# A streaming GELU-multiply: first tile loaded and stored in two pieces, GELU written to the output tile, whole-tile instructions elsewhere, activations pinned behind stores

## The chip, the cores and the metric

One core of one Trainium2 chip. The metric is the time on the device in microseconds (us), median of several runs; lower is better. The span, from the first to the last instruction, is 1.7 to 2.6 us shorter than the time of the same run.

## The reference

```python
x = randn(32, 512, 2048)  # float32
x1, x2 = x[..., :1024], x[..., 1024:]
gelu_x1 = 0.5 * x1 * (1 + erf(x1 / sqrt(2)))
return gelu_x1 * x2
```

134.2 MB are read and 67.1 MB written, with one GELU and one multiply for each output element.

## The kernel before

The rows are cut into 16 tiles: 128 partitions, 8 rows of 2048 columns each, so 8.39 MB in and 4.19 MB out. Both pools have two buffers. SP's queue issues the loads and the last two tiles' stores; ACT's queue issues the other stores.

```python
def load(i):
    x_tile = xpool.tile([P, R, dim], x.dtype, name="x_tile")
    nc.sync.dma_start(out=x_tile, in_=x_t[i])
    return x_tile
...
ahead = [load(0), load(1)]
for i in range(n_tiles):
    x_tile = ahead.pop(0)
    o_tile = opool.tile([P, R, half], out.dtype, name="o_tile")
    last = i == n_tiles - 1
    for lo, hi in ((0, 1), (1, 2), (2, 4), (4, 8)) if last else ((0, 4), (4, 8)):
        rows = slice(lo, hi)
        nc.scalar.activation(
            out=x_tile[:, rows, :half], in_=x_tile[:, rows, :half], func=GELU
        )
        nc.vector.tensor_mul(
            out=o_tile[:, rows, :],
            in0=x_tile[:, rows, :half],
            in1=x_tile[:, rows, half:],
        )
        if last and hi % 4 == 0:
            store(nc.sync, i, o_tile, slice(hi - 4, hi))
    if not last:
        store(nc.sync if i == n_tiles - 2 else nc.scalar, i, o_tile, slice(0, R))
    if i + 2 < n_tiles:
        ahead.append(load(i + 2))
```

A tile framework adds the semaphores, and it may choose the order of instructions on an engine where the data allow it.

## Time and profile before

| | before |
|---|---|
| time, median of 3 runs | 471.61 us |
| span of the profiled run | 470.1 us |
| ACT busy, DVE busy | 25%, 30% |
| bytes moved | 201.3 MB, 428 GB/s over the span |
| distance of tile starts in the middle | 29.0 us |

The prediction shows the page's lines. In the timeline of the kernel before, the columns are start, duration, engine, line, operation, output<-input, shapes, count and, in brackets, the idle time before it with what ended it:

```profile
74.42 7.12 ACT L55 ACTIVATE x_tile<-x_tile 128x4096 f32<-128x4096 f32 x2 [22.10 <-DMA x_tile<-in_x_dram]
78.07 8.76 DVE L58 TENSOR_TENSOR o_tile<-x_tile 128x4096 f32<-128x4096 f32 x2 [20.46 <-ACT x_tile L55]
86.86 0.36 ACTq L46 DMA_DIRECT2D out_dram<-o_tile  x1
```

One tile is 12.4 us of compute, with the halves overlapped; then ACT sleeps until the next load has landed. The second view is stretches of 1 us around the first store, which was issued at 35.24 us. The last two columns are the DMA engines' busy share and GB/s:

```profile
36.00:37.00 1.00, 0.00 (x0) 0.00 (x0) 0.00 (x0) 1.00 2.42 1049
37.00:38.00 1.00, 0.00 (x0) 0.00 (x0) 0.00 (x0) 1.00 0.00 0
38.00:39.00 1.00, 0.00 (x0) 0.00 (x0) 0.00 (x0) 1.00 3.58 983
39.00:40.00 1.00, 0.00 (x0) 0.00 (x0) 0.00 (x0) 1.00 0.25 66
40.00:41.00 1.00, 0.00 (x0) 0.00 (x0) 0.00 (x0) 1.00 0.00 0
41.00:42.00 1.00, 0.00 (x0) 0.00 (x0) 0.00 (x0) 1.00 0.00 0
42.00:43.00 1.00, 0.00 (x0) 0.00 (x0) 0.00 (x0) 1.00 1.14 492
```

The view counts a packet's bytes where the packet starts, and the 16 engines run nearly in step, so stretches of 1 us show when each round of packets begins: 1049 GB/s for 1 us is 16 packets of 64 KB. The round of 36 us is followed after a little over 2 us by that of 38 us; that round is followed only near 42.5 us. The share is counted there too, and so says how long a packet took: 2.42 x 1 us x 16 engines / 16 packets are 2.4 us in the round of 36 us; 3.58 x 16 / 15 packets (983 GB/s) are 3.8 us in that of 38 us. One round took 3.8 us instead of 2.4: this is the dip, about 1.4 us on all 16 engines, that the prediction saw as 262 GB/s.

### The profile page before, as it was taken

What the parts mean: (1) busy time and instruction counts of PE and PEld (TensorE: products, weight loads), DVE (VectorE), ACT (ScalarE), POOL (GpSimd) and SP (SyncE); (2) the same over time, 40 slices, a digit from 0 to 9 for tenths busy, and PEclk for the clock granted to TensorE, in tenths of its full rate; (3) what the DMA queues carried; (4) which work ended last, traced back from release to release, by engine and by line L of the source; (5) the groups of instructions that cost most, each with busy time, mean ns of one, the idle gap of its engine ahead of it and who ended that gap; (6) DMA issues with size and microseconds to landing.
All of it is one profiled execution on the core that took longest, in us unless ns stands there. A gap on an engine that the chain in (4) does not pass through costs nothing.

```text
span 470.1 us, 217 instructions
## 1 busy us (share of the span) xinstructions
DVE 140.5 (30%) x34; ACT 115.4 (25%) x35; POOL 0.2 (0%) x4
## 2 busy tenths in 40 slices
DVE  0070703307043070420705106061150601507042
ACT  1051406024060230603206032060410605105060
POOL 0000000000000000000000000000000000000000
DMA  8999999999999999999999999999999999999988
GB/s 357 446 446 357 443 449 446 402 443 449 402 446 441 435 457 404 432 418 485 407 424 421 488 407 413 432 488 407 402 443 482 413 402 443 472 424 402 480 380 346
DMA packets 4754, 201.35 MB, mean 428 GB/s; under 512 B 528, under 2 KB 528, under 8 KB 528
## 3 DMA queue, kind: packets, MB, share of 16 engines
q1 hardware_dynamic: 2736, 142.61, 70.5%
q10 hardware_dynamic: 2016, 58.72, 28.9%
q14 instruction: 2, 0.02, 0.0%
HBM read 134.22 MB, written 67.11 MB: 428 GB/s over the span
## 4 chain that ended last, share of the span: by engine, by line
DMA 77%; DVE 14%; ACT 7%; issue 0%; ACTq 0%; SPq 0%
DMA x_tile<-in_x_dram 77%; DVE o_tile L58 14%; ACT x_tile L55 7%; ACTq L94 0%; SPq L42 0%; ACTq L55 0%
## 5 line engine op out<-in xcount | busy, mean ns | idle before, releaser
L58 DVE TENSOR_TENSOR o_tile<-x_tile 128x4096 f32<-128x4096 f32 (+2 forms) x34 | 140.5, 4171 | 321.2 <-ACT x_tile L55 321.2
L55 ACT ACTIVATE x_tile<-x_tile 128x4096 f32<-128x4096 f32 (+2 forms) x34 | 114.2, 3407 | 341.0 <-DMA x_tile<-in_x_dram 341.0
L55 ACT ACT_TABLE_LOAD x1 | 1.3, 1283 | 0.7 <-PEq L83 0.7
L83 POOL MEMSET const-bfloat16-1.0<- 128x1 bf16 x1 | 0.1, 102 | 0.0
L83 POOL MEMSET const-uint8-127<- 128x1 uint8 x1 | 0.1, 102 | 0.0
L83 POOL MEMSET const-float32-0.0<- 128x1 f32 x1 | 0.1, 99 | 0.2 <-issue 0.2
L83 POOL MEMSET const-float32-1.0<- 128x1 f32 x1 | 0.1, 99 | 0.0
## 6 DMA issues: line engine op xcount, KB each, us to landing
out_dram<-o_tile ACTq DMA_DIRECT2D x14, 4096.0 KB, 41.6
out_dram<-o_tile SPq DMA_DIRECT2D x1, 4096.0 KB, 24.8
out_dram<-o_tile SPq DMA_DIRECT2D x2, 2048.0 KB, 8.0
x_tile<-in_x_dram SPq DMA_DIRECT2D x16, 45.4
```

What stands on the lines that cost most here:

```text
L55: nc.scalar.activation(out=x_tile[:, rows, :half], in_=x_tile[:, rows, :half], func=GELU)
L58: nc.vector.tensor_mul(out=o_tile[:, rows, :], in0=x_tile[:, rows, :half], in1=x_tile[:, rows, half:],)
L83: nc = _bacc.Bacc("TRN2", target_bir_lowering=False, num_devices=1)
```

## The change

The intent: get the first store out sooner, use fewer and larger instructions in the middle, and keep ACT from putting the next GELU ahead of a store that it has to issue.

```diff
     def load(i):
-        nc.sync.dma_start(out=x_tile, in_=x_t[i])
+        for rows in (slice(0, 4), slice(4, 8)) if i == 0 else (slice(0, 8),):
+            nc.sync.dma_start(out=x_tile[:, rows, :], in_=x_t[i][:, rows, :])
...
-        for lo, hi in ((0, 1), (1, 2), (2, 4), (4, 8)) if last else ((0, 4), (4, 8)):
+        pieces = i == 0 or last
+        steps = ((0, 2), (2, 4), (4, 8)) if pieces else ((0, 8),)
+        for lo, hi in steps:
             rows = slice(lo, hi)
-            nc.scalar.activation(
-                out=x_tile[:, rows, :half], in_=x_tile[:, rows, :half], func=GELU
+            tc.keep_in_program_order(
+                nc.scalar.activation(
+                    out=o_tile[:, rows, :], in_=x_tile[:, rows, :half], func=GELU
+                )
             )
             nc.vector.tensor_mul(
                 out=o_tile[:, rows, :],
-                in0=x_tile[:, rows, :half],
+                in0=o_tile[:, rows, :],
                 in1=x_tile[:, rows, half:],
             )
-            if last and hi % 4 == 0:
-                store(nc.sync, i, o_tile, slice(hi - 4, hi))
-        if not last:
+            if pieces and hi % 4 == 0:
+                store(nc.sync if last else nc.scalar, i, o_tile, slice(hi - 4, hi))
+        if not pieces:
```

## The prediction

> **What bounds the kernel now.** I read the page from the top: busy shares, slices, the chain that ended last, then the stretches of the trace and the start and the end in order of time. From the page of the kernel before:
>
> ```profile
> DVE 140.5 (30%) x34; ACT 115.4 (25%) x35; POOL 0.2 (0%) x4
> ...
> DMA  8999999999999999999999999999999999999988
> ...
> HBM read 134.22 MB, written 67.11 MB: 428 GB/s over the span
> ...
> DMA 77%; DVE 14%; ACT 7%; issue 0%; ACTq 0%; SPq 0%
> ...
> out_dram<-o_tile ACTq DMA_DIRECT2D x14, 4096.0 KB, 41.6
> out_dram<-o_tile SPq DMA_DIRECT2D x1, 4096.0 KB, 24.8
> out_dram<-o_tile SPq DMA_DIRECT2D x2, 2048.0 KB, 8.0
> x_tile<-in_x_dram SPq DMA_DIRECT2D x16, 45.4
> ```
>
> The reader sees two compute engines that sleep for 70% and more of the span, and a DMA row that stands at 8 or 9 in every slice. The chain of waits gives 21% to DVE and ACT: it goes tile load, GELU, multiply, next load that waits for the buffer. Read alone this suggests that a shorter compute stage would pay. But a load that is released by a multiply does not then start to move: it queues behind the load before it. That is why it takes 45.4 us to land although 8.39 MB at 434 GB/s are 19.3 us. So I asked for the stretches between tile starts:
>
> ```profile
> 45.20:103.30 58.10, 17.52 (x4) 14.24 (x4) 0.00 (x0) 1.00 1.00 434
> 103.30:161.20 57.90, 17.52 (x4) 14.25 (x4) 0.00 (x0) 1.00 1.00 434
> ...
> 277.30:335.20 57.90, 17.52 (x4) 14.24 (x4) 0.00 (x0) 1.00 1.00 434
> ```
>
> The last two columns are the DMA engines' busy share and GB/s: 1.00 and 434 in each pair of tiles. One tile is 8.39 MB in and 4.19 MB out, 12.58 MB, and 12.58 MB / 434 GB/s = 29.0 us, exactly the distance of the tile starts. The middle is bound by the DMA engines' rate, and its compute is free.
>
> What is left is at the edges. All 201.33 MB at 434 GB/s take 463.9 us; the span is 470.1, so **only 6.2 us in all are not transfer at full rate**. Where they are:
>
> ```profile
> 2.00:38.00 36.00, 8.76 (x2) 7.13 (x3) 0.00 (x0) 1.00 0.96 413
> 38.00:42.00 4.00, 0.00 (x0) 0.00 (x0) 0.00 (x0) 1.00 0.96 262
> ...
> 449.80:458.00 8.20, 5.42 (x4) 7.31 (x4) 0.00 (x0) 1.00 0.98 421
> 458.00:467.00 9.00, 3.66 (x1) 0.00 (x0) 0.00 (x0) 1.00 1.00 428
> 467.00:470.00 3.00, 0.00 (x0) 0.00 (x0) 0.00 (x0) 1.00 0.27 115
> ```
>
> The start costs about 2 us (first load issued at 0.73 us, engines busy from about 2 us). From 38 to 42 us, just after the first store was issued (35.24 us), the engines are busy but move only 262 GB/s: (434-262) x 4 us = 0.69 MB, worth 1.6 us. After 467 us the last packets finish, the semaphore arrives and the program ends: about 2 us. From 449.8 to 467 us the engines are nearly full (421, then 428 GB/s): the last two stores (8.39 MB, 19.3 us) run back to back.
>
> **What the Trainium skill says.** "DMA: Bandwidth & Descriptors", section "Where 436 GB/s comes from", puts the ceiling of the 16 ports at 435.2 GB/s; the trace's 434 is that ceiling. The same section holds that for HBM transfers a limit of about 358 GB/s binds; the trace disagrees for this one core alone, and the measurement decides. The same page, "Queues, rings and completion order", says that each DMA engine takes turns between its queues, one packet at a time. The trace agrees: in a tile's period the load queue moves 8.39 MB and the store queue 4.19 MB, each in 128 data packets, and both stay busy. "VectorE: DVE Perf Modes", section "The TRN2 errata", gives (N+151)/0.96 ns for an fp32 tensor_tensor: for 8192 elements 8.69 us, an estimate; the trace's two halves sum to 8.77 us (4096 measured 4.42 us), so one instruction saves 0.15 us of DVE at most.
>
> **The change part by part.**
> (1) Load 0 in two halves. Today it lands at 22.8 us. The halves carry 4.19 MB, 9.7 us each, so the first lands near 13.1 us. GELU on 2 and 2 rows (1.9 us each, from the 2048-column row), multiplies of 2.3 us each: 13.1 + 1.9 + 2 x 2.3 = 19.6 us, then the first half-store is issued, 15.6 us sooner than today. But the DMA engines are at 434 GB/s in that time with loads 0 and 1. An earlier store only moves bytes that go anyway ahead of other bytes; nothing idle is filled. Second half: 22.8 + 3.6 + 4.4 = 30.9 us, so load 2 and the other half-store are issued near 31 us instead of 35.2 us, both behind a queue. Gain: 0, except if the 1.6 us of slow packets at the first store vanish; I see no reason why a first store at 20 us should not show the same. One more DMA issue costs 0.33 us of SP, before any need.
> (2) Stores of tile 0 in halves have packets of 16 KB a partition against the loads' 64 KB. If turns are by packet, store 0a takes a fifth of the rate, 8 turns of (2.4 + 0.6) us = 24 us. From about 25 us it ends near 47-48 us, with load 1; store 0b and load 2 then share alike, 24 us, to about 72 us. Working: per DMA engine 64 KB at 434/16 GB/s are 2.4 us, 16 KB are 0.6 us.
> (3) GELU to o_tile. Today ACT waits for the load alone, and DVE for the store of two tiles before. Now ACT waits for both. Today the store issued at 86.86 us lands 41.5 us later (128.4 us), ACT of the tile that reuses its buffer starts at 132.35: 4 us of slack. By (2) the new store 0b lands near 72 us, and load 2 too: **the slack falls to about nothing**, perhaps 1 us short. With both queues never empty, stores and loads of later tiles each take 29.0 us and the tie persists. A tile start delayed by 1 us delays the next issue, which has a dozen us in hand (next line), so the middle doesn't lengthen.
> (4) Whole-tile instructions in 14 tiles: GELU then multiply no longer overlap. Today load to store is 12.4 us (74.42 to 86.86); now 7.1 + 8.7 = 15.8 us, 3.4 us later. The queues hold work for longer: the load ahead lands a tile's period after, 29.0 us, leaving 13 us. The store queue's earlier store also lasts until about then. Cost 0.
> (5) Last tile in 2, 2, 4 rows instead of 1, 1, 2, 4. The first half-store needs 1.9 + 2.3 + 2.3 = 6.5 us against about 6.2 us, ready before the 9.7 us of store 14 are over. The last: GELU 7.3 us, less about 0.1 for one instruction fewer, then 4.4 us. End = start of the last GELU + 19.4 us, as today (449.89 to about 469.3), where both the store traffic (19.3 us) and this chain (11.8 us + 7.6 us from issue to landing) end together. This is the only place where the slack of (3) matters: if store 13 lands 1 us after load 15, the last GELU begins late. Bytes are conserved, so about half of it is real loss: 0.5 us.
> (6) The pinning of ACT's order: in the built programs ACT's order around the stores is the same as before. Cost 0.
>
> Sum: -0.1 (5), up to +0.1 for tile 0's smaller packets (which I take from the final slices' 428 against 434 GB/s: 8.39 MB of tile 0's load is 0.27 us at that ratio, as an upper bound), +0.5 from the tie at the end, between 0 and -1.6 from the first store's stall, which I rate a quarter likely to shrink: -0.4. Together 0 to +0.1 us. **I predict 471.5 us.**
>
> **Rivals.** *The earlier first store shortens the fill.* If tile 0 set the end, 15.6 us sooner would be worth up to that. For it: the chain puts DVE and ACT on the path at tile 1 (45.19 to 57.61). Against: load 1 keeps the DMA engines full through the fill, and a lower bound of 463.9 us of transfer plus 2 us of start and 2 us of end leaves 468 us of span. This would make it at best 469.5 us as timed, not faster by 2% (462.2), which is below the transfer time itself.
> *The new ACT wait becomes the bound.* If stores land well after loads, t(i) = landing of store i-2, and 16 us of unoverlapped compute enters the loop. For a closed loop the distance of two tiles would have to exceed 58 us: 15.8 us compute and a store alone at 1/3 rate, 29 us, are 45 us. So it stays hidden; only if stores got far less than a third would it bite. Store lag of 4 us would add 2 us at the end: 473.5 us.
> *DVE in place slows.* The multiply now reads and writes o_tile. If it lost even 30%, 8.8 us become 11.4 us, still inside the 13 us of (4); only the last multiply (4.4 us) would show, +1.3 us.
>
> **Range and chances.** The DMA floor fences the low side at about 469.5 us; the end's tie and a lagging store make the high side 473.5 us. Repeats of the kernel before lie within 0.3 us. Range 469.6 to 473.2. Faster by 2% would need 9.4 us and only 6.2 us aren't transfer: 1%. Slower by 2% needs a DMA queue to run dry in the middle: 2%. Within 2%: 97%.
>
> **What would show it.** The first half of load 0 lands near 13 us and the first store is issued near 20 us (1). Stretches of the middle still show 434 GB/s and tile starts 29.0 us apart (3, 4). ACT's longest waits are put down to stores as well as to loads (3), with multiplies of about 8.7 us and GELUs of about 7.0 us. The dip at the first store moves to about 22-28 us (1). The last GELU starts near 450 us and the span ends 19.4 us or a little more later (5). The prediction is wrong if a stretch in the middle falls well below 434 GB/s (a queue ran dry), or if the last GELU starts several us sooner.

## The result, and the profile after

The changed kernel took **471.11 us** (471.02 to 471.17, 6 runs), against 471.67 us (6 runs) of the kernel before in the same rounds. The ratio is 0.9986, with a 95% interval of 0.9973 to 0.9999. The span fell from 470.1 to 469.2 us.

The page of the changed kernel, engines and chain:

```profile
DVE 139.5 (30%) x20; ACT 114.2 (24%) x21; POOL 0.2 (0%) x4
...
DMA out_dram<-o_tile 62%; DVE o_tile L65 14%; ACT o_tile L61 12%; DMA x_tile<-in_x_dram 10%; ACTq L101 0%; SPq L45 0%
```

The chain has turned over: it was 77% waits for loads, now 62% are waits for stores. Its compute share grew from 21 to 26%. The time hardly moved. The list of waits of the changed kernel says the same from ACT's side (total, times, longest):

```profile
ACT o_tile L61 <- DMA out_dram<-o_tile: 303.6, 14, 22.1
ACT o_tile L61 <- DMA x_tile<-in_x_dram: 37.7, 3, 20.9
```

Its timeline, at the first tiles and at the end:

```profile
12.81 3.71 ACT L61 ACTIVATE o_tile<-x_tile 128x2048 f32<-128x2048 f32 x2 [10.80 <-DMA x_tile<-in_x_dram]
...
19.28 0.38 ACTq L49 DMA_DIRECT2D out_dram<-o_tile  x1
...
30.63 0.36 ACTq L49 DMA_DIRECT2D out_dram<-o_tile  x1
47.07 7.03 ACT L61 ACTIVATE o_tile<-x_tile 128x8192 f32<-128x8192 f32 x1 [20.94 <-DMA x_tile<-in_x_dram]
54.13 8.69 DVE L65 TENSOR_TENSOR o_tile<-o_tile,x_tile 128x8192 f32<-128x8192 f32 x1 [23.54 <-ACT o_tile L61]
62.86 0.36 ACTq L49 DMA_DIRECT2D out_dram<-o_tile  x1
71.62 7.03 ACT L61 ACTIVATE o_tile<-x_tile 128x8192 f32<-128x8192 f32 x1 [17.52 <-DMA out_dram<-o_tile]
...
449.07 7.21 ACT L61 ACTIVATE o_tile<-x_tile 128x2048 f32<-128x2048 f32 x3 [21.99 <-DMA out_dram<-o_tile]
```

The first store goes out at 19.28 us instead of 35.24. Compute to store is 15.8 us (47.07 to 62.86) instead of 12.4. Tile starts from 100.61 to 449.07 us are 29.0 us apart. The last GELU starts 0.8 us sooner than before (449.07, was 449.89), and from there to the end of the span it is 20.1 us, before 20.2. So by the tiles nearly the whole gain, 0.8 of 0.9 us, lies ahead of the last one.

Around the first store, stretches of 1 us of the changed kernel:

```profile
21.00:22.00 1.00, 0.00 (x0) 0.00 (x0) 0.00 (x0) 1.00 2.16 852
22.00:23.00 1.00, 0.00 (x0) 0.48 (x1) 0.00 (x0) 1.00 0.50 197
23.00:24.00 1.00, 0.00 (x0) 1.00 (x1) 0.00 (x0) 1.00 0.00 0
24.00:25.00 1.00, 0.00 (x0) 1.00 (x1) 0.00 (x0) 1.00 0.93 393
```

The 64 KB round that begins at 21 to 22 us took 2.7 us (2.16 x 16 / 13 packets), not 3.8. The dip became small, by about 1 us. But its size does not simply carry to the end. Summed over the packets of the two traces, the changed kernel is 1.06 us ahead in bytes moved at 45 us and only 0.45 us ahead at 449 us: over half of the gain is lost again in the middle, and the record does not show to what. The rest of the 0.9 us between the two spans comes after 467 us, where the last data packet ends at 468.92 us before and at 467.87 us now. That much is within the scatter of the kernel before: its other runs have spans of 469.5 to 470.7 us.

### The profile page after: what moved, and what is told of

It reads as the page before. It is cut to its first block, busy times and chain, and to the rows that moved or that the text cites. A ratio compares the mean times of both kernels' runs of the same rounds, so it can differ in the third digit from the quotient of the medians.

```text
span 469.2 us, 182 instructions
## 1 busy us (share of the span) xinstructions
DVE 139.5 (30%) x20; ACT 114.2 (24%) x21; POOL 0.2 (0%) x4
## 4 chain that ended last, share of the span: by engine, by line
DMA 72%; DVE 14%; ACT 12%; ACTq 0%; SPq 0%; issue 0%
DMA out_dram<-o_tile 62%; DVE o_tile L65 14%; ACT o_tile L61 12%; DMA x_tile<-in_x_dram 10%; ACTq L101 0%; SPq L45 0%
## 5 line engine op out<-in xcount | busy, mean ns | idle before, releaser
L65 DVE TENSOR_TENSOR o_tile<-o_tile,x_tile 128x8192 f32<-128x8192 f32 (+2 forms) x20 | 139.5, 6985 | 321.2 <-ACT o_tile L61 321.2
L61 ACT ACTIVATE o_tile<-x_tile 128x8192 f32<-128x8192 f32 (+2 forms) x20 | 112.9, 5661 | 341.3 <-DMA out_dram<-o_tile 303.6
```

The costliest lines, as they stand in the source:

```text
L61: nc.scalar.activation(out=o_tile[:, rows, :], in_=x_tile[:, rows, :half], func=GELU)
L65: nc.vector.tensor_mul(out=o_tile[:, rows, :], in0=o_tile[:, rows, :], in1=x_tile[:, rows, half:],)
```

## The experiments

Besides the two kernels, twelve experimental ones ran. Times are medians; the ratios are to the kernel before in the same rounds.

| run | time us | ratio (95% interval) | span us |
|---|---|---|---|
| changed kernel | 471.11 | 0.9986 (0.9973 to 0.9999) | 469.2 |
| e10, tile 0 alone | 471.42 | 0.9995 (0.9983 to 1.0007) | 469.5 |
| e3, GELU to output tile alone | 471.75 | 1.0002 (0.9990 to 1.0014) | 470.3 |
| e4, whole tiles alone, not pinned | 478.54 | 1.0149 (1.0134 to 1.0164) | 475.6 |
| e11, whole tiles alone, pinned | 471.66 | 0.9999 (0.9986 to 1.0013) | 469.6 |
| e1, load 0 whole again | 471.65 | 1.0008 (0.9992 to 1.0024) | 469.4 |
| e2, store 0 whole again | 472.54 | 1.0019 (1.0007 to 1.0031) | 469.3 |
| e7, store 0 in halves in the kernel before | 472.58 | 1.0028 (1.0016 to 1.0040) | 470.7 |
| e8, load 2 issued later | 472.05 | 1.0005 (0.9993 to 1.0017) | 469.5 |
| e9, multiplies cut away | 470.63 | 0.9978 (0.9966 to 0.9990) | 468.5 |
| e5, GELU twice | 488.18 | 1.0354 (1.0331 to 1.0376) | 487.8 |
| e6, GELU thrice | 514.26 | 1.0873 (1.0784 to 1.0962) | 510.4 |
| e13, GELU twice from tile 2 on | 470.72 | 0.9980 (0.9966 to 0.9993) | 469.0 |

### One part at a time

**Tile 0 alone** (e10), in the kernel before:

```diff
-        nc.sync.dma_start(out=x_tile, in_=x_t[i])
+        for rows in (slice(0, 4), slice(4, 8)) if i == 0 else (slice(0, 8),):
+            nc.sync.dma_start(out=x_tile[:, rows, :], in_=x_t[i][:, rows, :])
...  # tile 0 worked in rows ((0, 2), (2, 4), (4, 8)), stored in two halves
```

> The kernel before with tile 0 alone changed: its load in two halves, its rows worked as 2, 2, 4, its store in two halves. Theory A (the small gain comes from tile 0: a shorter dip in the DMA rate at the first store): as the changed kernel, about 0.5 us under the kernel before, span near 469.2 us. Theory B (the gain comes from whole-tile instructions or the last tile): no difference from the kernel before, span near 470.1 us.

Measured 471.42 us and a span of 469.5 us. The dip is as small as in the changed kernel (the round at 21.6 us took 2.7 us), so tile 0's pieces are what made it small. The time leans to theory A, but its interval includes no gain at all, and the kernel before had spans from 469.5 to 470.7 us in the same rounds. A difference of 0.1% can't be split further with these runs.

**GELU to the output tile alone** (e3):

```diff
-                out=x_tile[:, rows, :half], in_=x_tile[:, rows, :half], func=GELU
+                out=o_tile[:, rows, :], in_=x_tile[:, rows, :half], func=GELU
...
-                in0=x_tile[:, rows, :half],
+                in0=o_tile[:, rows, :],
```

> The kernel before with GELU written to the output tile, nothing else. Theory A: ACT's new wait for the store of two tiles before is over about 4 us before the load lands (store landings 4 us ahead of tile starts), so 0 us of difference within 0.3 us and no ACT wait put down to stores. Rival C (the new wait costs): 1 us or more longer.

As theory A has it: 471.75 us, and all 16 of ACT's tile waits are put down to loads. The new wait is there and free.

**Whole-tile instructions alone** (e4), without the pin:

```diff
-        for lo, hi in ((0, 1), (1, 2), (2, 4), (4, 8)) if last else ((0, 4), (4, 8)):
+        for lo, hi in ((0, 1), (1, 2), (2, 4), (4, 8)) if last else ((0, 8),):
```

> The kernel before with one GELU and one multiply for each tile but the last. Theory A: stores and loads are issued 3.4 us later in each tile, into queues that still hold 13 us of work: 0 us within 0.3 us. Rival (the compute on the chain of waits counts): 14 tiles by 3.4 us, up to 48 us longer.

Both were wrong: 478.54 us, 1.5% slower. The timeline of this run shows where:

```profile
108.26 8.69 DVE L58 TENSOR_TENSOR o_tile<-x_tile 128x8192 f32<-128x8192 f32 x1 [20.30 <-ACT x_tile L55]
116.98 29.32 SPq L42 DMA_DIRECT2D x_tile<-in_x_dram  x2
130.19 7.03 ACT L55 ACTIVATE x_tile<-x_tile 128x8192 f32<-128x8192 f32 x1 [21.96 <-DMA x_tile<-in_x_dram]
130.22 16.12 ACTq L46 DMA_DIRECT2D out_dram<-o_tile  x2
```

The multiply ends at 116.95 us and SP issues the next load at once, at 116.98. The store goes out only at 130.22, after the next tile's GELU was handed to ACT, and that GELU waited for its load. In the built program ACT's order at this point is GELU, GELU, store, store; the framework had put a GELU ahead of a store, in three places (the late pairs of stores go out at 130.22, 246.94 and 365.30 us). From 161 us on the stretches show 422 to 425 GB/s instead of 434.

**The same, pinned** (e11):

```diff
+            tc.keep_in_program_order(
                 nc.scalar.activation(...)
+            )
```

> The kernel before with whole-tile instructions, as in the run that took 478.5 us, and with GELU pinned in program order besides. In that run ACT's order had the next tile's GELU ahead of the store in some tiles (at 130.2 us), so that the store went out 13 us late. Theory D (that order is the loss): with the pin every store follows its multiply, and the time is that of the kernel before within 0.5 us, 471.1 to 472.1 us. Rival (whole-tile instructions as such cost, by 3.4 us later issues): 478 us again.

471.66 us, as theory D has it. The store now follows its multiply:

```profile
108.33 8.69 DVE L60 TENSOR_TENSOR o_tile<-x_tile 128x8192 f32<-128x8192 f32 x1 [20.30 <-ACT x_tile L56]
117.06 0.36 ACTq L46 DMA_DIRECT2D out_dram<-o_tile  x1
```

So the loss of 7 us was ACT's order. Whole-tile instructions as such cost nothing, and the pin is what makes them free. In the changed kernel built without the pin, the order again has GELU, GELU, store, store, in two places; that kernel was not run.

### Does the wait for stores hurt?

**Load 0 whole again** (e1) makes the stores lag on purpose:

```diff
-        for rows in (slice(0, 4), slice(4, 8)) if i == 0 else (slice(0, 8),):
+        for rows in (slice(0, 8),):
```

> The changed kernel with load 0 whole again (tile 0's stores stay in halves). By packet turns the first half-store then starts near 33 us, takes 24 us, the second ends near 82 us, while load 2 lands near 70 us: GELU of tile 2 must wait some 12 us for the store. Theory A (queues have enough work to ride over this): within 1.5 us of the changed kernel, 471 to 472.6 us. Rival C (ACT's wait for stores becomes the bound when stores lag): the 12 us show in the time, 480 us or more.

The timeline of this run:

```profile
81.67 7.03 ACT L61 ACTIVATE o_tile<-x_tile 128x8192 f32<-128x8192 f32 x1 [29.28 <-DMA out_dram<-o_tile]
...
101.17 7.03 ACT L61 ACTIVATE o_tile<-x_tile 128x8192 f32<-128x8192 f32 x1 [12.48 <-DMA out_dram<-o_tile]
```

ACT waited for the store until 81.67 us; turn-taking packet by packet had given 82. Yet the next tile starts at 101.17 us, within 0.6 us of the changed kernel's, and the time is 471.65 us (one of six runs took 474.2). Rival C falls: a delay of 10 us in the compute made about 0.5 us at the end, by the medians, and not the 8 us or more of rival C.

**Store 0 in halves in the kernel before** (e7), after the whole tile's steps:

```diff
-            store(nc.sync if i == n_tiles - 2 else nc.scalar, i, o_tile, slice(0, R))
+            for rows in (slice(0, 4), slice(4, 8)) if i == 0 else (slice(0, R),):
+                store(nc.sync if i == n_tiles - 2 else nc.scalar, i, o_tile, rows)
```

> The kernel before with store 0 cut in two halves that are both issued at 35.2 us, together with load 2: 16 KB packets, no earlier than before. If packet size makes the dip, it shrinks to a few tenths of a us and the time falls by 0.5 to 1 us (less what a store lagging behind the loads takes at the end); if the issue beside a load makes it, the dip stays and the time is that of the kernel before or more.

The edit missed its aim: the framework issued the first half at 30.76 us, as soon as its rows were done, so "both at 35.2 us" was not tested. The run was 472.58 us, slower by 0.28%, and shows the one place where lagging stores count. At the end GELU of the last tile starts at 445.57 us, but the multiplies wait for a store until 454.07:

```profile
445.57 7.31 ACT L55 ACTIVATE x_tile<-x_tile 128x1024 f32<-128x1024 f32 x4 [21.89 <-DMA x_tile<-in_x_dram]
454.07 8.90 DVE L58 TENSOR_TENSOR o_tile<-x_tile 128x1024 f32<-128x1024 f32 x4 [15.44 <-DMA out_dram<-o_tile]
```

Stores 8 us behind loads at the last tile: about 1 us at the end (from 449 to 467 us the DMA engines move 392 GB/s, 422 in the kernel before). The prediction's rival had put half of the lag there.

### What made the dip smaller?

**Store 0 whole again** (e2):

```diff
-            if pieces and hi % 4 == 0:
-                store(nc.sync if last else nc.scalar, i, o_tile, slice(hi - 4, hi))
-        if not pieces:
+            if last and hi % 4 == 0:
+                store(nc.sync, i, o_tile, slice(hi - 4, hi))
+        if not last:
```

> The changed kernel with tile 0's store whole: 32 KB packets, issued near 31 us together with load 2. It tells apart what shortens the dip at the first store. Theory P (packet size, or issue beside a load): the dip of some 1.5 us is back and the time is 0.5 to 1 us over the changed kernel. Theory Q (the earlier first store as such): the dip stays small, time as the changed kernel within 0.3 us. Store 0 should land near 64 to 66 us, some 6 us ahead of load 2, so ACT waits for loads again.

The dip is back: a round of load packets starts at 33 to 35 us and nothing more until 37 us. Each of its packets took 3.6 us (2.02 x 16 / 9):

```profile
33.00:34.00 1.00, 0.00 (x0) 0.00 (x0) 0.00 (x0) 1.00 2.02 590
```

ACT's 17 waits are put down to loads again, as expected. The dip speaks for theory P. The time, 472.54 us, is 1.4 us over the changed kernel, more than theory P allows; its six runs spread from 471.45 to 473.27, and the profiled one has the dip and yet a span of 469.3 us. So the time does not measure what the dip costs.

**Load 2 issued later** (e8), by a GELU that nobody reads:

```diff
+        if i == 0:
+            tc.keep_in_program_order(
+                nc.scalar.activation(
+                    out=x_tile[:, :, :half], in_=x_tile[:, :, half:], func=GELU
+                )
+            )
         if i + 2 < n_tiles:
             ahead.append(load(i + 2))
```

> The kernel before with one more GELU over tile 0's own buffer after its store is issued, so that load 2 is issued near 42.5 us and store 0 alone at 35.2 us, with 32 KB packets as before. If the dip comes from both being issued at once, it is gone and the time is up to 1 us shorter; if it comes from the first 32 KB store packets, it stays at 38 to 42 us and the time is that of the kernel before. Load 1 lands at 45 us, so the load queue doesn't run dry.

Load 2 went out at 42.57 us and store 0 alone at 35.09. The round of 36 us took 3.4 us:

```profile
36.00:37.00 1.00, 0.00 (x0) 1.00 (x1) 0.00 (x0) 1.00 3.37 1049
```

Most of the dip stays, and the time, 472.05 us, is that of the kernel before within its interval. Issuing both at once is thus not the main cause. The traces of all these runs together say more. Each round below is one of 64 KB load packets; "lost" is what all load packets from 20 to 45 us took beyond 2.42 us each, on the average engine:

| kernel | load 0 | store 0 | slowed rounds, us | lost, us |
|---|---|---|---|---|
| before | whole | whole, with load 2 | 3.8 | 1.5 |
| e8 | whole | whole, alone | 3.4 | 1.2 |
| e2 | halves | whole, with load 2 | 3.6 | 1.2 |
| e7 | whole | halves | 2.9 and 3.0 | 1.0 |
| e1 | whole | halves | 2.8 and 3.0 | 1.0 |
| e10 | halves | halves | 2.7 | 0.4 |
| changed | halves | halves | 2.7 | 0.4 |

A half-store, of 16 KB packets, slows its round less than a whole one of 32 KB; but two half-stores slow two rounds, unless load 0 is in halves too and the first of them goes out at 19 us. Why the second half-store hardly slows a round then (a store while load 0's half-size packets were still in the queue, perhaps) stays open.

### How much compute is free?

**Multiplies cut away** (e9), wrong results:

```diff
+            cols = slice(0, half if pieces else 16)
             nc.vector.tensor_mul(
-                out=o_tile[:, rows, :],
+                out=o_tile[:, rows, cols],
...
```

> The changed kernel with the multiplies of tiles 1 to 14 cut to 16 of 1024 columns: wrong results on purpose. The multiply (8.7 us) is then gone from each pass of the chain of waits, where DVE has 14% of the span. Theory A (the DMA engines bound the middle): 0 us within 0.5 us. Rival (the chain's compute share is worth its time): 7 links of 8.4 us, some 59 us shorter.

470.63 us: 0.5 us under the changed kernel's median. The chain of waits had 14% of the span on DVE, 65 us; taking out the seven multiplies that make 61 us of it is worth 0.5 us. The bound is the DMA engines.

**GELU twice and thrice** (e5, e6), in tiles 1 to 14, same result:

```diff
-            tc.keep_in_program_order(
+            for _ in range(1 if pieces else 2):  # e6: 3
+                tc.keep_in_program_order(
```

> The changed kernel with the GELU of tiles 1 to 14 done twice (same result). Compute from tile start to the next issues becomes 15.8 + 7.0 = 22.8 us, against 29.0 us a tile: the margin falls from 13 to 6 us. Theory A: no difference from the changed kernel within 0.5 us. Rival (unoverlapped compute costs): 14 x 7 us = 98 us, or at least several us.

> The same with GELU three times: 15.8 + 14.1 = 29.9 us, which is over the 29.0 us of a tile's transfers; ACT also waits in its own order for each multiply before it issues the store. Theory A: now the queues run dry and the compute loop sets the time: about 30.3 us a tile, 14 x 1.3 us, so some 15 to 25 us longer, 486 to 496 us. If it is still free, the margin I worked out (13 us) is wrong.

Twice was not free: 488.18 us. Theory A was wrong, and the rival's "several us" came true, though, as e13 will show, not for its reason. Thrice took 514.26 us, beyond the expected 496. The timeline of e5 shows that tile 1 issues its store at 70.05 us (its load goes with it), and already at 71.64 us the next tile starts, for which all earlier transfers have landed:

```profile
70.05 0.36 ACTq L49 DMA_DIRECT2D out_dram<-o_tile  x1
71.64 14.09 ACT L62 ACTIVATE o_tile<-x_tile 128x8192 f32<-128x8192 f32 x2 [10.34 <-DMA out_dram<-o_tile]
```

Both queues ran dry there, since tile 2 follows tile 1 by 24.4 us instead of 29: by the packets of the trace, the last of load 2 and store 0 end at 70.7 to 71.0 us, and the first of the new load start at 71.0 to 72.2 us. Afterwards every stretch is slow, though tiles issue 7 to 11 us ahead of the next start. Was it this lead that was too short, or the one dry moment?

**GELU twice from tile 2 on** (e13):

```diff
-            for _ in range(1 if pieces else 2):
+            for _ in range(2 if 2 <= i < n_tiles - 1 else 1):
```

> The changed kernel with GELU twice in tiles 2 to 14 only; in the run with it from tile 1 on (488.2 us) both queues ran dry once, at 70 us, because tile 1 had less time. Theory L (lead: each tile issues its load and store only some 6 to 7 us before the queues need them, and that is too late each time): still 1.0 to 1.2 us a tile, 483 to 488 us. Rival S (the one dry start spoilt the rest): 471 to 473 us.

470.72 us: theory S. The same stretch of e5 and then of e13, both with GELU twice:

```profile
70.00:449.00 379.00, 104.33 (x13) 179.69 (x26) 0.00 (x0) 1.00 1.00 415
```

```profile
70.00:449.00 379.00, 113.00 (x13) 183.04 (x27) 0.00 (x0) 1.00 1.00 434
```

With a lead of 6.1 us (issue at 94.35 us, next tile at 100.48) the DMA engines keep 434 GB/s. In e5, with leads no shorter, they stay at 415 for the rest of the run although they count as busy. The packets show where that goes. Here are the load queue's packets, MB and share of the 16 engines from 110 to 440 us, of e5 and then of e13:

```profile
q1 hardware_dynamic: 1570, 91.36, 67.9%
```

```profile
q1 hardware_dynamic: 1632, 95.42, 66.7%
```

For each 64 KB, this is 2.57 us in e5 and 2.42 in e13. In e5, 28% of the load packets took over 2.5 us (2.95 on average); in e13, none did, and the store packets took 1.2 us in both. Until the dry moment of e5 all 16 engines start each round within 0.4 us; after it they are out of step and never fall in again. Of the 18.6 us between the spans of e5 and the changed kernel, 16.2 are such longer packets and 2.5 are engines without a packet. In e6, of 41.2 us, 16.4 are longer packets and 24.9 idle engines, so that the compute loop cost what was expected of it and the longer packets the rest. The loss of e4 is of the same kind: its store queue also ran dry (stores issued 13 us late), and 17% of its load packets took over 2.5 us, none in e11. Why the packets take longer, whether being out of step does it, and why one dry moment is never recovered from, is open.

No run beats the changed kernel clearly; e13 and e9 lie within its interval.

## Why the prediction was right

It was right: 471.11 us against 471.5, inside 469.6 to 473.2, and within 2%. By its own steps:

- **The bound.** Right. 434 GB/s in the middle and 29.0 us a tile in both kernels; the cut multiplies (e9) show that DVE's share of the chain is worth about nothing.
- **(1) Earlier first store.** Right on the times: first half in use at 12.81 us (13.1 predicted), stores issued at 19.28 and 30.63 us (19.6 and about 31), and sending a store 16 us sooner saved no such time. The dip was the mis-sized term. I saw no reason why it should shrink, and gave that a quarter of a chance and 0.4 us; it shrank by about 1 us, of which some 0.5 us was left near the end.
- **(2) Packet turns.** Right: tile 1 starts at 47.07 us (47 to 48 predicted), tile 2 at 71.62 us (about 72), with store and load together. The first is part luck: "from about 25 us" and 24 us make 49. In the trace the first round of load 1 goes alone at 21.7 us, and the turns begin at 24.4. That both queues move 128 packets in a tile's period is no evidence of turns, since each tile has as many of each. The packets are: in the middle 16 of 64 KB (2.42 us each) and 16 of 32 KB (1.21 us each) start in turn, and eight such pairs make 29.0 us.
- **(3) GELU's new wait.** Right: the slack went from 4 us to nothing, 14 of 17 waits are now for stores, and the middle did not lengthen. The 0.5 us that I set down for the end did not come: from the last GELU to the end is 20.1 us, before 20.2.
- **(4) Whole tiles.** Right for the changed kernel: 15.8 us, cost 0. (Two halves of 4.42 us sum to 8.84 us, not 8.77, which is the time from the first's start to the second's end in the chain; the saving of 0.15 us goes with 8.84.)
- **(5) Last tile.** -0.1 us predicted, and 20.2 to 20.1 us seen, with one profile of each. That the end comes 19.4 us after the last GELU was misread: it was 20.2 us before, up to 470.1 us.
- **(6) The pin, "cost 0".** True of the two kernels as built, but read too shallowly: I compared their ACT orders, found them the same, and filed the pin as idle. Without it part (4) alone costs 7 us (e4 against e11). It is the condition of (4).
- **Rivals.** The wait as the bound fell (e1). The in-place multiply did not slow: 8.69 us for 8192 elements, which is what the formula of "VectorE: DVE Perf Modes" gives, though the page states it for an add.
- **The number.** Closer than its sum. The terms give 0 to +0.1 us, so 471.6 to 471.7 us; 471.5 does not follow from them. And two terms were off: no 0.5 us came at the end, and the dip gave more than was set down for it. What was shown is that the DMA engines' rate sets the time and that nothing in the change could move it far; the last half us was not foreseen.

The gain of 0.6 us between the medians is too small to split. Its interval ends 0.01% from zero; the smaller dip is a cause of the right size, and tile 0 alone (e10) shows the dip but no gain clear of noise. That the dip is the cause is not shown.

## What to carry to other kernels

When the DMA engines run at their rate through the middle, count what is not transfer (here 6.2 us of 470) before hoping for more from earlier stores or fewer instructions. Here queues that always held work hid compute and new waits, so that the chain of waits turned over without the time moving; but see that no queue runs dry even once, which cost 17 us in e5. And look at the order on an engine that both computes and issues stores: a GELU placed ahead of a store, in three places, cost 7 us, more than all the rest of this change could gain.

## What the Trainium skill lacked or had wrong

- "DMA: Bandwidth & Descriptors", section "Where 436 GB/s comes from", says without a condition that for HBM transfers the limit of about 358 GB/s binds; the same page's measurements keep that figure for two cores streaming at once. One core alone held 434 GB/s of loads and stores together here, for 350 us.
- The same page has nothing on the first store into a stream of loads: one round of 64 KB packets took 3.8 us instead of 2.4 in the kernel before, and 2.7 us in the changed one.
- No page that I read tells that two queues which ran dry once can stay slow: 415 GB/s against 434 for the rest of the run, with 64 KB packets of 2.57 us on average against 2.42 (e5 against e13).
- "VectorE: DVE Perf Modes" checks its fp32 tensor_tensor formula, for an add, at 512 and 2048 elements; at 8192 it gives 8.69 us, and 8692 ns were measured for the multiply here.
